# A gate's products spread over the last inverse of a DeltaNet layer, with other pools and planner costs, and an early table load

## The chip, the cores and the metric

The kernel runs on one core of a Trainium2 chip. The metric is the device time of one execution in microseconds. "TensorE" (PE in the profile) does matrix products, "DVE" is VectorE, "ACT" is ScalarE, "POOL" is GpSimd, and "SP" is SyncE, whose queue issues nearly all DMA transfers. PEld is TensorE's weight load, which overlaps its products.

## The reference: what is computed

One layer of a streaming encoder on a sequence of 1024 frames of width 1024, then a final RMSNorm. All is in float32. Cut to what matters:

```python
h = rmsnorm(x, norm_mix_g)
proj = h @ w_in            # columns of all heads, and two merge gates
# Branch A: gated DeltaNet, 8 heads of 128: causal conv + SiLU on q, k, v, chunks of tokens
lower = where(strict, beta * (k k^T) * decay, 0)
sol = triangular_solve(lower, rhs, unit_diagonal=True)      # the kernel forms the inverse itself
# then a scan over the chunks with a state of 128 x 128 per head
# Branch B: GLA, 4 heads, chunked, with its own scan
merged = sigmoid(gate_a) * (o_a @ w_branch_gdn) + sigmoid(gate_b) * (o_b @ w_branch_gla)
x = x + merged @ w_out
# cross attention over 256 memory tokens
m = rmsnorm(mem, norm_mem_g)
k, v = m @ wk, m @ wv
x = x + softmax(q k^T / 16) v @ wo
# MLP
x = x + square(relu(rmsnorm(x) @ w1)) @ w2
return rmsnorm(x, norm_final_g)
```

## The kernel before

**Products.** A float32 operand is split into a rounded part (`hi`, by ACT) and a remainder (`lo`, by DVE or POOL): this is `split` (lines 584 and 585 of the profile). One product of two such operands is then three products of TensorE, `hi*hi`, `hi*lo`, `lo*hi` (`mm3`, lines 544, 546 and 548). Most large products use a scheme of seven products in place of eight on 2 by 2 blocks (`wino`), with operands 0 to 6 that lie in the slots B0a, B0b, A1a, A1b, A0a, B1a, B1b. A few are plain float32 products, which the profile shows as two records each.

**Order.** Two things set it. First, dense products are pushed as generators on a queue (`push`), and dependent work calls `fill(n)` to put the next n dense products at that place of the program, or `until(name)` and `drain()` to put all of them up to a name there. Secondly, a planner (`Plan`, with costs of every operation in `Op`) reads the whole program and fixes an order on each engine: the operation with the least latest start first on DVE, ACT, POOL and SP; on TensorE, of those that are ready, the one that stands first in the program. So a later product can be put into a gap in which the earlier ones aren't ready. The order is fixed before the run; each engine then works strictly through its own. TensorTensor operations with two operands can go to DVE or to POOL, as the planner's costs say.

**Phases.** `phase0` loads the memory tokens (`mem_piece`, line 702: ACT scales each of eight blocks of 256 tokens by the norm's gain into `mf`), forms keys and values and the normalised x. `phase_gla` is branch B. `phase_gdn` is branch A: four pairs of heads p = 0 to 3; each has convolutions of k, q, v (`push_conv`: 48 products, then ACT line 1247, three DVE steps at line 1250 and a SiLU at line 1251), `gdn_subst` on DVE (ending in two transposes, lines 1367 and 1371, into `PF` and `PT`), `gdn_queries`, `gdn_v` (line 616 transposes, line 1427), `gdn_inverse` and `gdn_scan`. `gdn_inverse` is a chain of small products (32 by 32 at lines 1394 and 1403, 64 by 64 at lines 1410 and 1417) with copies by ACT and DVE between them and a `fill(nfill)` at four places. For the first three pairs `nfill` is `GF[6]`, 8, and the queue holds the next pair's convolutions.

For the last pair there is no next pair. The queue ends with gate 5 (`push_gate`: one load of weights, then 48 products in two halves, each with a tanh by ACT and a store). The fills of 24 and 16 behind the two `gdn_v` and then `drain()` put its products in front of the inverse; `ectx.close(); wctx.close()` free the phase's pools; `begin_merge` opens the pools of the merge (`plate`, `big2` with B0a and B0b, `w4` with the weights) and loads the operands 0 to 4 of the first merge product `yb`. Then come the inverse and the scan, and behind them in the program `yb`, of which the planner puts products into the scan's gaps. A slot A1a, A1b, A0a is free for its merge operand only when the gate's products, which read the normalised x in it, are through.

**Pools.** Pools are stacked from both ends of on-chip memory ("left" and "right"); a pool that lies over the addresses of a closed one waits for the last use of what was there. `pge` (right) held k0, kdt0, NT0, dm and acc of the phase; `w1` (right, outside it) holds raw weights and a ring of four split ones (`wop`).

Of the kernel before, what the change touches and what calls it, by code (L numbers as in the profile page):

```python
# [18 lines left out]
P = 128  # L19
# [24 lines left out]
KP = 2  # L44
LOVU = (5,)
LOV = (0, 2, 5)
GLG, GN = 0, (0, 0, 0, 1)
ZA = "z"
DH = ((0, 1, 2, 3), (4, 5, 6, 7), (), ())
XF = (4, 12, 10, 8)  # L50
# [32 lines left out]
class Op:  # L83
# [5 lines left out]
    def __init__(self, ins, flex):  # L89
# [27 lines left out]
        if scan:  # L117
            vec = 65 + wide * 2.08
        elif ins.opcode == "StreamTranspose":
            vec = (830 if rough else 90) + wide * 1.042  # L120
        elif ins.opcode == "Reciprocal" or n <= 16 and wide <= 16:
            vec = 82
        pool = {"Memset": 20 + n * 0.875, "TensorScalarAffineSelect": 140 + n * 0.89, "TensorCopy": 140 + n * 0.9}
        self.costs = costs = {"vector": vec, "gpsimd": 245 + n * 1.98 if sums else pool.get(ins.opcode, 100 + n)}
        if sums and n <= 16:
            costs["gpsimd"] = 330 + 160 * n
        if ins.opcode == "DMACopy":
            self.dma, self.cost, self.lat = True, 60, 2600
            self.bytes = n * 4 * outs[0].ap[0][1]
        elif eng == "tensor":  # L130
            m = size(ins_[0])
            if ins.is_transpose:
                self.cost = m * 0.85
            elif ins_[0].dtype == F32R:
                self.cost = m * 0.4427 + (4 if m < HALF else 0)
            else:
                self.cost = max(m, size(ins_[1])) * 1.667 + 8
            self.lat = 205
        elif eng == "scalar":
            self.cost = (60 if psum(ins_[0]) else 95) + n * (1.71 if rough else 0.834) + 90 * min(cols, 1) + 90 * (len(outs) > 1)  # L140
            self.lat, self.own = 140, 130
        else:
            self.port = eng == "gpsimd" or two
            self.place(eng)

# [320 lines left out]
class Layer:  # L466
# [151 lines left out]

    def slot(self, name, shape=(NB, HALF), dt=F32R):

        pool = self.bp if name[0] == "A" else self.bp2 if name[1] == "0" else self.bp3
        return self.til(pool, (P,) + shape, name, dt, bufs=1)

    def colsum(self, out, src, n):
# [37 lines left out]
    def consts(self):  # L662
        nc, a = self.nc, self.a
        cp = self.cp = self.pool(self.ctx, "const", "left")
        self.ident = self.til(cp, [P, P], "ident")
        make_identity(self.tc.nc, self.ident)
        self.mhalf = self.til(cp, [P, 16], "mhalf")
        nc.vector.memset(self.mhalf, -0.5)
        self.ones = self.til(cp, [P, 1], "ones")
        nc.vector.memset(self.ones, 1.0)  # L670
        cols = self.til(cp, [P, 56], "cols")
        nc.scalar.dma_start(cols, a["cols"])
        self.g_mix, self.g_x = cols[:, 0:8], cols[:, 8:16]
        self.g_mem, self.g_mlp = cols[:, 16:24], cols[:, 24:32]
        self.b_gate, self.g_fin = cols[:, 32:36], cols[:, 48:56]
        self.a_log, self.dt_bias = cols[:, 39:40], cols[:, 40:41]

        gh = self.til(cp, [P, 3], "ghalf")
        nc.vector.tensor_scalar(gh, cols[:, 36:39], 0.5, None, MUL)
        self.g_gdn, self.g_gla = gh[:, 0:1], gh[:, 1:3]  # L680
        self.convw = self.til(cp, [P, 24, 4], "convw")
        nc.sync.dma_start(self.convw, a["convw"])
        self.tm = self.til(cp, [P, NB, 2, GH], "tm")
        self.geg = self.til(cp, [P, NB, GH], "geg")
        self.gge, self.kf = (self.til(cp, [P, GH, NB], n) for n in ("gge", "kf"))
        self.pad(cp, 160)


    def phase0(self, xp, gp):
        nc, a = self.nc, self.a  # L690
        with ExitStack() as ctx:
# [6 lines left out]

            def mem_piece(i):
                self.load(mraw[:, 2 * i:2 * i + 2], a["memT"][:, 2 * i:2 * i + 2])  # L700
                for k in (2 * i, 2 * i + 1):
                    nc.scalar.activation(mf[:, k], mraw[:, k], AF.Copy, scale=self.g_mem[:, k:k + 1])

            def split_mem():
                self.split(mf, mT[:, 0], mT[:, 1], nc.vector)
# [450 lines left out]
    def phase_gla(self):  # L1156
        nc, a = self.nc, self.a
        with ExitStack() as ctx:
# [31 lines left out]
            for h in range(LH):  # L1190
# [31 lines left out]
                self.push_z(sp, h + 1, after if ZA == "z" else None)  # L1222
                if h < LH - 2:
                    self.push_gates(sp, 5 + h)
                if h == LH - 2:
                    for i in range(5, 5 + GLG):
                        self.push_gate(i, lambda src: self.wpart(src, [NB, P], nc.vector), sp, "ex", EXB, T)
                self.fill(FG if h == 1 else FE)


# [294 lines left out]
    def phase_gdn(self, wctx):  # L1525

        nc, a = self.nc, self.a
        with ExitStack() as lctx:
            ectx, sctx = ExitStack(), ExitStack()
            sv = self.pool(lctx, "pgv", "left", bufs=2)  # L1530
            sq = self.pool(sctx, "pgl", "left", bufs=2)
            sp = self.pool(ectx, "pge", "right", bufs=2)
# [1 line left out]
                self.til(sv, [P, T], tag, bufs=2)  # L1534
            for tag in ("k1", "kdt1", "NT1", "q"):
                self.til(sq, [P, T], tag, bufs=2)
            for tag in ("k0", "kdt0", "NT0", "dm", "acc"):
                self.til(sp, [P, T], tag, bufs=2)
            self.til(sq, [P, T], "X", bufs=2)
            self.subTA = self.til(sq, [P, 16, 64], "subTA", bufs=1)  # L1540
            nc.gpsimd.memset(self.subTA, 0.0)
# [2 lines left out]

            def push_keys(hs):
                par = hs[0] // 2 % 2
                sts = [{"pool": sq if par else sp, "tag": lambda t: f"{t}{par}"} for _ in hs]
                for h, st in zip(hs, sts):
                    st["k"] = self.til(st["pool"], [P, NB, P], st["tag"]("k"), bufs=2)
                    conv(f"k{h}", GH + h, a["w_gdn"][3 * h], lambda acc, st=st: st["k"])  # L1550
                return sts
# [6 lines left out]
                self.gdn_keys(sp, sq, hs[1], sts[1])  # L1558
                return self.gdn_subst(sp, sq, sts)

            gates = iter(range(5 + GLG, 6))
            getw = lambda src: self.wpart(src, [NB, P])
            last = None
            sts = push_keys((0, 1))
            for st, h in zip(sts, (0, 1)):
# [1 line left out]
            for p in range(GH // 2):  # L1567
# [9 lines left out]
                nxt = None  # L1577
                if p < GH // 2 - 1:
                    nxt = push_keys((2 * p + 2, 2 * p + 3))
                for _ in range(GN[p]):  # L1580
                    self.push_gate(next(gates), getw, sp)
                if last:
                    for h, st in last:
                        self.gdn_norm(sv, st)
# [9 lines left out]
                self.fill(GF[3])  # L1594
                self.gdn_queries(sv, sp, sts[1])
                self.until(f"v{hs[1]}")
                self.gdn_v(sv, sts[0])
                self.fill(GF[4])
                self.gdn_v(sv, sts[1])
                self.fill(GF[5])  # L1600
                if nxt:
                    self.until(f"k{hs[1] + 2}")
                else:
                    self.drain()
                    ectx.close()
                    wctx.close()
                    ob = self.begin_merge()
                self.gdn_inverse(sts, PF, GF[6])
                if nxt:
                    ns = (2 * p + 2, 2 * p + 3)  # L1610
                    for st, h in zip(nxt, ns):
                        self.load_decay(sp, h, st)
# [16 lines left out]

    def begin_merge(self):  # L1630

        sp = self.plate = self.pool(self.ctx, "plate", "right")
        self.pad(sp, 32, ([P, HALF], "e", 3), ([P, HALF], "acc", 2), ([P, HALF], "q", 4))
        self.bp2 = self.pool(self.ctx, "big2", "right")
        for n in ("B0a", "B0b"):
            self.slot(n)
        self.wp = self.pool(self.ctx, "w4", "right")
        self.queue_w()
        self.fetch_w()
        ob = {"SL": ("B0a", "B0b", "A1a", "A1b", "A0a", "B1a", "B1b")}  # L1640
        for p in range(5):
            self.load_op(sp, ob, p, lambda p, k: self.obd[p][:, k], range(4), None)
        return ob

    def big3(self, ob):

# [1005 lines left out]
```

## Time and profile before

| what | value |
|---|---|
| median of 3 runs | 2131.04 us (2130.86 to 2133.01) |
| the profiled execution | 2133.65 us, span 2131.8 us |
| TensorE's mean granted clock | 0.994 of full speed |
| busy: TensorE, DVE, ACT, POOL | 2105.4, 1694.6, 1124.6, 198.3 us |

The span runs from the first to the last instruction that the profile shows. A row of busy time by stretch has the stretch, its length, then for PE, PEld, DVE, ACT and POOL the busy microseconds and the number of instructions, then TensorE's granted clock as a share of full speed, the mean busy share of the 16 DMA engines, and GB/s. A row of the timeline has start and length in us, engine, line, operation, output and inputs; in brackets the idle time before it and what ended that.

### The profile page before, as it was taken

To read this page: it belongs to the slowest core of one execution; us is meant where nothing else is said; L and a number is where in the kernel's file an instruction comes from. 1 tells how busy PE (TensorE), PEld (TensorE's weight loads), DVE (VectorE), ACT (ScalarE), POOL (GpSimd) and SP (SyncE) were. 2 spreads that over 40 slices of the span, in tenths; PEclk is the share of its full clock that TensorE was granted. 3 is DMA by queue.
4 is the path that set the end of the run, shared out by engine and by line. 5 is a ranking of instruction groups with operands and counts; after the bars stand their busy time and mean duration, and the time that the engine had idled before them with its cause. 6 is when DMAs were issued, how large, how long until landed. Compare 5 with 4: busy or idle time off the path is not lost.

```text
span 2131.8 us, 31725 instructions
## 1 busy us (share of the span) xinstructions
PE 2105.4 (99%) x11308; PEld 1771.7 (83%) x11308; DVE 1694.6 (79%) x3051; ACT 1124.6 (53%) x2244; POOL 198.3 (9%) x199
## 2 busy tenths in 40 slices
PE   8999999999999999999999999999999999999998
PEld 7898887988888888888888888888888888887877
DVE  7979698879768787777899858788979777577766
ACT  6555454454454747475643446676655556444433
POOL 1102001000001121212010001100200000000001
PEclk9999999999999999999999999999999999999999
DMA  7523333223241030303498653466454556688852
GB/s 279 197 70 111 129 120 114 80 89 120 74 140 60 11 124 12 124 11 118 151 307 299 216 198 112 143 198 220 122 157 141 163 158 183 198 276 267 273 180 91
DMA packets 147040, 321.70 MB, mean 151 GB/s; under 512 B 16056, under 2 KB 19512, under 8 KB 146880
## 3 DMA queue, kind: packets, MB, share of 16 engines
q1 hardware_dynamic: 143984, 315.44, 45.1%
q10 hardware_dynamic: 2896, 4.22, 0.6%
q8 instruction: 89, 1.46, 0.3%
q14 instruction: 71, 0.58, 0.1%
HBM read 223.10 MB, written 96.50 MB: 150 GB/s over the span
## 4 chain that ended last, share of the span: by engine, by line
PE 86%; DVE 6%; DMA 3%; ACT 2%; issue 1%; POOL 0%; SPq 0%; POOLq 0%; DVEq 0%; ACTq 0%
PE pd L544 20%; PE pd L546 20%; PE pd L548 20%; PE ps L544 5%; PE ps L546 5%; PE ps L548 5%; PE ps L616 2%; DMA raw<-in_w_dram 1%; DMA rawa<-ad 1%; DMA e<-ad 1%; PE ps L1452 1%; PE pd L767 1%; PE ps L1459 1%; PE ps L1469 1%; PE ps L1311 1%
## 5 line engine op out<-in xcount | busy, mean ns | idle before, releaser
L584 ACT ACTIVATE wop<-raw 128x512 fp32r<-128x512 f32 (+1 forms) x535 | 355.9, 671 | 527.2 <-PE pd L548 253.8
L585 DVE TENSOR_TENSOR wop<-raw,wop 128x512 fp32r<-128x512 f32 (+1 forms) x512 | 373.6, 734 | 122.7 <-ACT wop L584 115.6
L548 PE MATMUL pd<-A1a,wop 128*128 128x512 f32 x376 | 148.6, 395 | 0.0
L544 PE MATMUL pd<-A1a,wop 128*128 128x512 f32 x376 | 147.1, 392 | 0.0
L546 PE MATMUL pd<-A1b,wop 128*128 128x512 f32 x356 | 139.7, 392 | 0.0
L548 PE MATMUL pd<-t,wop 128*128 128x512 f32 x312 | 124.0, 398 | 0.1
L544 PE MATMUL pd<-t,wop 128*128 128x512 f32 x312 | 121.8, 391 | 2.1 <-ACT wop L584 1.9
L546 PE MATMUL pd<-A1a,wop 128*128 128x512 f32 x312 | 122.8, 394 | 0.2
L546 PE MATMUL pd<-t,wop 128*128 128x512 f32 x312 | 121.7, 390 | 0.0
L544 PE MATMUL pd<-A1b,wop 128*128 128x512 f32 x292 | 115.4, 395 | 0.0
L548 PE MATMUL pd<-A1b,wop 128*128 128x512 f32 x292 | 114.7, 394 | 0.0
L1250 DVE SCALAR_TENSOR_TENSOR acc<-cin,convw,acc 128x1024 f32<-128x1024 f32 x72 | 94.4, 1312 | 15.5 <-ACT acc L1248 14.9
L544 PEld LDWEIGHTS pd<-A1a,wop 128*128 128x128 f32 x376 | 70.7, 188 | 14.3
L548 PEld LDWEIGHTS pd<-A1a,wop 128*128 128x128 f32 x376 | 70.7, 188 | 13.9
L544 PE MATMUL pd<-B0a,wop 128*128 128x512 f32 x196 | 77.1, 394 | 2.5 <-ACT wop L584 2.0
L544 PE MATMUL pd<-A0a,wop 128*128 128x512 f32 x196 | 79.4, 405 | 0.0
L546 PEld LDWEIGHTS pd<-A1b,wop 128*128 128x128 f32 x356 | 66.9, 188 | 13.4 <-DVE A1b L585 0.5
L546 PE MATMUL pd<-A0a,wop 128*128 128x512 f32 x196 | 78.0, 398 | 0.0
L548 PE MATMUL pd<-B0a,wop 128*128 128x512 f32 x196 | 77.4, 395 | 0.0
L548 PE MATMUL pd<-A0a,wop 128*128 128x512 f32 x196 | 77.2, 394 | 0.0
L546 PE MATMUL pd<-A0b,wop 128*128 128x512 f32 x184 | 73.2, 398 | 0.0
L548 PE MATMUL pd<-A0b,wop 128*128 128x512 f32 x184 | 72.6, 395 | 0.0
(660 smaller groups left out, 6025.8 us busy)
## 6 DMA issues: line engine op xcount, KB each, us to landing
raw<-in_w_dram SPq DMA_DIRECT2D x120, 256.0 KB, 4.0
raw<-in_w_dram SPq DMA_DIRECT2D x32, 512.0 KB, 4.4
e<-ad SPq DMA_DIRECT2D x63, 256.0 KB, 4.8
raw<-in_w_gdn_dram SPq DMA_DIRECT2D x24, 512.0 KB, 5.5
ad<-q SPq DMA_DIRECT2D x45, 256.0 KB, 4.6
rawa<-ad SPq DMA_DIRECT2D x42, 256.0 KB, 4.7
A0b<-tgd SPq DMA_DIRECT2D x32, 256.0 KB, 5.1
raw<-in_w_gate_dram SPq DMA_DIRECT2D x15, 512.0 KB, 3.7
```

The source lines that it names most:

```text
L544: nc.tensor.matmul(out, lh, rh, start=first and i == 0, stop=False, skip_group_check=more)
L546: nc.tensor.matmul(out, lh, rl, start=False, stop=False, skip_group_check=more)
L548: nc.tensor.matmul(out, ll, rh, start=False, stop=last and i == n - 1, skip_group_check=more)
L584: nc.scalar.activation(hi, raw, AF.Copy)
L585: (lo_eng or nc.gpsimd).tensor_tensor(lo, raw, hi.bitcast(F32), SUB)
L616: self.nc.tensor.transpose(pt[:, i * P:(i + 1) * P], s, self.ident)
L767: nc.tensor.matmul(pt[:, j * MEM:(j + 1) * MEM], w[k // 4][:, k % 4, js], mf[:, k], start=k == 0, stop=k == NB - 1)
L1250: nc.vector.scalar_tensor_tensor(acc, cin[:, 1 + i:1 + i + T], cw[:, i:i + 1], acc, MUL, ADD)
L1311: nc.tensor.matmul(pt[:, i * P:(i + 1) * P], kc, kc, start=True, stop=True)
L1452: nc.tensor.matmul(py[:, 0:P], st["NT"][:, c, :], zh[h], start=True, stop=True)
L1459: nc.tensor.matmul(pd[h][:, 0:P], st["kd"][:, c, :], dl[h], start=True, stop=True)
L1469: nc.tensor.matmul(po[:, 0:P], st["AT"][:, c, :], dl[h], start=True, stop=True)
```

## The change

The costs of some operations in the planner are changed. The gate's products get their fills inside the last inverse (`GL`, four fills of 12), its split weights and its tanh output a pool of their own. k0, kdt0 and NT0 get a pool that closes when the last pair begins. The pools of the merge and its operand 0 are opened in front of the inverse as before, operands 1 to 4, with the slot B0b in a new pool, behind it. At the beginning ACT runs a copy of one column at once, before mem arrives, and DVE scales every second block of mem. The branch with `GLG` in `phase_gla` had an empty range and is taken out.

```diff
-GLG, GN = 0, (0, 0, 0, 1)
+GL = (0,0,12)
...
         elif ins.opcode == "StreamTranspose":
-            vec = (830 if rough else 90) + wide * 1.042
+            vec = 60 + wide * 1.93 if rough else 90 + wide * 1.042
...
-        pool = {"Memset": 20 + n * 0.875, "TensorScalarAffineSelect": 140 + n * 0.89, "TensorCopy": 140 + n * 0.9}
-        self.costs = costs = {"vector": vec, "gpsimd": 245 + n * 1.98 if sums else pool.get(ins.opcode, 100 + n)}
+        pool = {"Memset": 20 + n * 0.875, "TensorScalarAffineSelect": 140 + n * 1.29, "TensorCopy": 300 + n * 2}
+        self.costs = costs = {"vector": vec, "gpsimd": 320 + n * 1.98 if sums else pool.get(ins.opcode, 100 + n)}
...
+            if outs[0].ap[0][1] < P:
+                self.cost += 117
...
+            if eng == "vector" and outs[0].ap[0][1] < P:
+                costs["vector"] += 117
...
-        pool = self.bp if name[0] == "A" else self.bp2 if name[1] == "0" else self.bp3
+        pool = self.bp if name[0] == "A" else self.bp3 if name[1] == "1" else self.bp2 if name == "B0a" else self.bp4
...
         nc.scalar.dma_start(cols, a["cols"])
+        nc.scalar.activation(self.mhalf[:, 15:16], self.ones, AF.Copy)
...
             def mem_piece(i):
                 self.load(mraw[:, 2 * i:2 * i + 2], a["memT"][:, 2 * i:2 * i + 2])
-                for k in (2 * i, 2 * i + 1):
-                    nc.scalar.activation(mf[:, k], mraw[:, k], AF.Copy, scale=self.g_mem[:, k:k + 1])
+                nc.scalar.activation(mf[:, 2 * i], mraw[:, 2 * i], AF.Copy, scale=self.g_mem[:, 2 * i:2 * i + 1])
+                nc.vector.tensor_scalar(mf[:, 2 * i + 1], mraw[:, 2 * i + 1], self.g_mem[:, 2 * i + 1:2 * i + 2], None, MUL)
...
-            for tag in ("k0", "kdt0", "NT0", "dm", "acc"):
+            for tag in ("dm", "acc"):
                 self.til(sp, [P, T], tag, bufs=2)
+            pk = self.pool(kctx, "pgk", "right", bufs=2)
+            for tag in ("k0", "kdt0", "NT0"):
+                self.til(pk, [P, T], tag, bufs=2)
...
-            gates = iter(range(5 + GLG, 6))
-            getw = lambda src: self.wpart(src, [NB, P])
...
                 if p < GH // 2 - 1:
                     nxt = push_keys((2 * p + 2, 2 * p + 3))
-                for _ in range(GN[p]):
-                    self.push_gate(next(gates), getw, sp)
+                else:
+                    kctx.close()
+                    gp = self.pool(gctx, "pgg", "left")
+
+                    def getw(src):
+                        raw = self.til(self.wp, [P, NB, P], "raw", bufs=RAWS)
+                        hi, lo = (self.til(gp, [P, NB, P], n, F32R, bufs=1) for n in ("ghi", "glo"))
+                        self.load(raw, src)
+                        self.split(raw, hi, lo)
+                        return hi, lo
+
+                    self.push_gate(5, getw, gp, "tg", 2)
...
                 self.until(f"v{hs[1]}")
+                if not nxt:
+                    self.fill(1)
                 self.gdn_v(sv, sts[0])
-                self.fill(GF[4])
+                self.fill(GF[4] if nxt else GL[0])
                 self.gdn_v(sv, sts[1])
-                self.fill(GF[5])
+                self.fill(GF[5] if nxt else GL[1])
                 if nxt:
                     self.until(f"k{hs[1] + 2}")
                 else:
-                    self.drain()
                     ectx.close()
                     wctx.close()
                     ob = self.begin_merge()
-                self.gdn_inverse(sts, PF, GF[6])
-                if nxt:
+                self.gdn_inverse(sts, PF, GF[6] if nxt else GL[2])
+                if not nxt:
+                    self.drain()
+                    gctx.close()
+                    self.begin_ops(ob)
+                else:
...
     def begin_merge(self):
...
-        for n in ("B0a", "B0b"):
-            self.slot(n)
+        self.slot("B0a")
...
-        for p in range(5):
-            self.load_op(sp, ob, p, lambda p, k: self.obd[p][:, k], range(4), None)
+        self.load_op(self.plate, ob, 0, lambda p, k: self.obd[p][:, k], range(4), None)
         return ob
+
+    def begin_ops(self, ob):
+
+        self.bp4 = self.pool(self.ctx, "big4", "right")
+        for p in range(1, 5):
+            self.load_op(self.plate, ob, p, lambda p, k: self.obd[p][:, k], range(4), None)
```

More of the change, by code (lines that the diff above doesn't have):

```diff
@@ L1224, in phase_gla @@
                     self.push_gates(sp, 5 + h)
-                if h == LH - 2:
-                    for i in range(5, 5 + GLG):
-                        self.push_gate(i, lambda src: self.wpart(src, [NB, P], nc.vector), sp, "ex", EXB, T)
                 self.fill(FG if h == 1 else FE)
@@ L1528, in phase_gdn @@
         with ExitStack() as lctx:
-            ectx, sctx = ExitStack(), ExitStack()
+            ectx, sctx, kctx, gctx = (ExitStack() for _ in range(4))
             sv = self.pool(lctx, "pgv", "left", bufs=2)
@@ L1546, in push_keys @@
                 par = hs[0] // 2 % 2
-                sts = [{"pool": sq if par else sp, "tag": lambda t: f"{t}{par}"} for _ in hs]
+                sts = [{"pool": sq if par else pk, "tag": lambda t: f"{t}{par}"} for _ in hs]
                 for h, st in zip(hs, sts):
@@ L1630, in begin_merge @@
     def begin_merge(self):
-        sp = self.plate = self.pool(self.ctx, "plate", "right")
-        self.pad(sp, 32, ([P, HALF], "e", 3), ([P, HALF], "acc", 2), ([P, HALF], "q", 4))
+        self.plate = self.pool(self.ctx, "plate", "right")
+        self.pad(self.plate, 32, ([P, HALF], "e", 3), ([P, HALF], "acc", 2), ([P, HALF], "q", 4))
         self.bp2 = self.pool(self.ctx, "big2", "right")
-        for n in ("B0a", "B0b"):
-            self.slot(n)
+        self.slot("B0a")
         self.wp = self.pool(self.ctx, "w4", "right")
```

## The prediction

> **What bounds the kernel.** I read the page first, then TensorE's waits, then the busy time by stretch, and last the timeline of the two places that the diff touches.
>
> ```profile
> PE 2105.4 (99%) x11308; PEld 1771.7 (83%) x11308; DVE 1694.6 (79%) x3051; ACT 1124.6 (53%) x2244; POOL 198.3 (9%) x199
> PE 86%; DVE 6%; DMA 3%; ACT 2%; issue 1%; POOL 0%; SPq 0%; POOLq 0%; DVEq 0%; ACTq 0%
> PE pd L544 <- ACT wop L584: 6.7, 5, 2.2
> PE pd L767 <- ACT mf L702: 1.6, 1, 1.6
> PE ps L1410 <- DVE subTA L1404: 1.5, 1, 1.5
> ```
>
> TensorE is busy 99% of the span and is 86% of the chain that ended last. The diff takes no product away, so the change can pay only where TensorE stands idle or runs at a lower clock. Of the waits listed (us in total, times, longest), the third lies in the last inverse, one of the five of the first as well, and the second at the beginning: the change reaches those.
>
> The clock is the larger matter. These rows (TensorE's clock behind the POOL column, as a share of full speed) cut the time around the last inverse into stretches of 3.41 us:
>
> ```profile
> 991.40:1003.90 12.50, 12.50 (x65) 10.36 (x63) 8.83 (x9) 2.84 (x4) 3.02 (x2) 1.00 0.25 84
> 1003.90:1005.05 1.15, 1.15 (x34) 0.87 (x34) 0.00 (x0) 0.76 (x2) 0.10 (x1) 1.00 0.00 0
> 1005.05:1008.46 3.41, 1.83 (x89) 1.59 (x84) 1.28 (x3) 3.17 (x9) 0.00 (x0) 1.00 0.77 232
> 1008.46:1011.87 3.41, 2.88 (x64) 2.63 (x64) 0.56 (x2) 2.40 (x6) 0.00 (x0) 0.50 0.96 383
> 1011.87:1015.28 3.41, 1.98 (x10) 1.33 (x11) 3.35 (x6) 1.75 (x4) 0.00 (x0) 0.50 0.60 206
> 1015.28:1018.70 3.42, 3.42 (x38) 3.42 (x37) 1.80 (x4) 1.74 (x3) 0.00 (x0) 0.50 0.37 111
> 1018.70:1022.12 3.42, 3.42 (x17) 2.92 (x16) 1.89 (x3) 0.89 (x2) 0.00 (x0) 0.50 0.00 0
> ```
>
> Until 1003.9 the gate's 48 products keep TensorE full. Then the inverse stands bare: 1.58 + 0.53 + 1.43 = 3.54 us idle, and four stretches, 13.66 us, at half clock. The first three inverses, against the last:
>
> ```profile
> 698.20:711.10 12.90, 12.90 (x248) 10.68 (x247) 8.28 (x11) 9.08 (x18) 0.10 (x1) 1.00 0.11 38
> 803.70:816.60 12.90, 12.90 (x248) 10.75 (x248) 8.28 (x11) 9.08 (x18) 0.10 (x1) 1.00 0.13 40
> 909.10:922.10 13.00, 13.00 (x248) 10.81 (x248) 8.31 (x12) 9.08 (x18) 0.10 (x1) 1.00 0.12 41
> 1004.20:1020.40 16.20, 12.67 (x229) 11.22 (x229) 7.89 (x15) 9.81 (x21) 0.05 (x1) 0.63 0.57 196
> ```
>
> An inverse has 32 + 48 + 16 + 16 small float32 products in the code, which leave two records each, 224 in all; a dense product leaves one. The first three have 24 dense products between its steps (three fills of 8), TensorE full and the clock whole; the last has five, and 0.63.
>
> **The change, part by part.** *The gate's products beside the inverse.* Same 48 products, same place in the dense queue; only the fills move: none behind the two gdn_v, then four times 12 in the inverse. The weights are still requested before it. A dense product takes the step between these two starts, 0.23 us:
>
> ```profile
> 1003.41 0.39 PE L544 MATMUL pd<-A1a,wop 128*128 128x512 f32 x1
> 1003.64 0.39 PE L546 MATMUL pd<-A1a,wop 128*128 128x512 f32 x1
> ```
>
> So an inverse's own work at full clock is 12.9 - 24 x 0.23 = 7.4 us. Now 1004.2 to 1020.4 holds that and five products of the merge: 7.4 + 5 x 0.23 = 8.55 us of work in 16.2 us. That is 7.65 us to win, and half of the 1.72 us at half clock from 1020.4 to 1022.12, 0.86: **8.5 us**, if TensorE stays full from 991.4. A second way, all half-clock busy time counted half: 3.54 + 11.70 / 2 = 9.4, the upper end. The lower end is the idle time alone, 3.5. I take 8.5, since three inverses with this cover show it.
>
> Is the work there to be interleaved? Behind the last convolution's products (until 991.4) stands its chain on DVE and ACT:
>
> ```profile
> 991.38 1.07 DVE L1367 STREAM_TRANSPOSE X<-Pm 128x512 f32<-128x512 f32 x1
> 995.19 1.06 DVE L1371 STREAM_TRANSPOSE X<-X 128x512 f32<-128x512 f32 x1
> 999.30 1.06 ACT L1251 ACTIVATE acc<-acc 128x1024 f32<-128x1024 f32 x1 [0.85 <-DVE acc L1250]
> 1000.41 1.09 PE L616 MATMUL ps<-ident,acc 128*128 128x128 f32 x8
> ```
>
> The gate now hides that chain until 1000.4. With the gate's products spread out, the cover is the inverse itself: its first operand exists at 992.45 and its second transpose, put behind a convolution step at 995.19, at 996.25 even if it isn't moved forward. In the worst case some 20 products (4.6 us / 0.23) go before the inverse really starts; 28 are left, more than the 24 that sufficed three times. DVE has 17.7 us of work in 991.4 to 1022.12 (the seven rows), 79% of the 22.2 us that remain, its mean over the span; ACT 13.55, 61%. So neither becomes the bound there. Scan start moves from 1020.4 to about 1012.
>
> *Pools.* k0, kdt0 and NT0 get a pool that closes before the last pair; the split gate weights get a pool of their own and no longer pass through the four-deep weight ring. That lets the merge's weights and B0a be opened before the inverse. Against it: the operand in B0b opens only when the gate's last product and tanh are through, near 1012, and its ACT splits wait for that with the scan's evictions behind them on ACT. Cost taken as zero, because the scan had other work first:
>
> ```profile
> 1020.41 0.63 PE L1452 MATMUL ps<-v,NT 128*128 128x128 f32 x2
> 1032.31 0.39 PE L544 MATMUL pd<-B0b,wop 128*128 128x512 f32 x1
> 1022.12:1053.20 31.08, 31.08 (x208) 27.49 (x208) 28.75 (x74) 25.39 (x84) 1.45 (x2) 1.00 0.39 129
> 1022.12:1053.20 31.08, 19.89 (x63) 10.65 (x64) 2.06 (x3) 1.21 (x2) 1.00 0.39 129
> ```
>
> The last row is the dense products alone: 63 in the scan. B0b was first read 11.9 us after the scan's start; from 1012 that is 1024, 12 us after the pool opens. Its four loads and the twelve of the operands behind it are issued behind the inverse on SP's queue instead of before it; they had 9 us of lead on the scan and now have about none. If the cover is gone, see the last rival. A gain can come too: B0a ready early.
>
> *Durations.* The planner's costs change for DVE's transposes, short-partition copies and POOL's work; no instruction gets faster by that, but every engine's order from end to end is drawn anew. What it can move is the stalls elsewhere, the largest of them here, where an idle 2.23 us costs half of the next 3.42 us too:
>
> ```profile
> 1940.30:1943.71 3.41, 1.18 (x6) 0.68 (x5) 2.13 (x4) 1.24 (x3) 0.00 (x0) 1.00 0.98 299
> 1943.71:1947.13 3.42, 3.42 (x9) 2.68 (x10) 3.42 (x6) 2.05 (x5) 0.00 (x0) 0.50 0.79 267
> ```
>
> That stall is worth 2.2 + 1.7 = 3.9 us. It may go, or another like it may come: plus or minus 3.9, taken as zero.
>
> *The beginning.*
>
> ```profile
> 4.12 1.28 ACT L702 ACT_TABLE_LOAD   x1 [4.12 <-DMA mraw<-in_memT_dram]
> 5.42 1.71 ACT L702 ACTIVATE mf<-mraw,cols 128x256 f32<-128x256 f32 x4
> 5.98 1.13 PE L767 MATMUL pd<-mf,raw 128*128 128x256 f32 x4 [1.55 <-ACT mf L702]
> 8.47 3.81 PE L767 MATMUL pd<-mf,raw 128*128 128x256 f32 x9 [1.36 <-DMA raw<-in_wk_dram]
> 9.96 0.69 DVE L733 TENSOR_TENSOR mraw<-mraw 128x512 f32<-128x512 f32 x1 [2.12 <-ACT mf L702]
> 10.30 0.91 ACT L702 ACTIVATE mf<-mraw,cols 128x256 f32<-128x256 f32 x2 [0.37 <-DMA mraw<-in_memT_dram]
> ```
>
> The load of 1.28 us goes in front of mem's arrival, so the first products start some 1.2 us earlier. But the next ones wait for weights until 8.47: late next is that DMA, and most is lost again. The last mem piece lands at 10.30 and its two scalings (0.91) now run side by side: 0.45 earlier for what follows. DVE gets four scalings of at most 0.69 each, in its waits. I take **0.4 us**, between 0 and 1.3 (the load's 1.28).
>
> **Sum.** 8.5 + 0.4 = 8.9 us. The profiled execution took 2133.65 us (span 2131.8), 2.6 above the median of the three runs, 2131.04; I take the gain off the median: 2131.0 - 8.9 = **2122.1 us**.
>
> **Rivals.** (a) Only the idle time comes back: 2131.0 - 3.5 - 0.4 = 2127.1. For it: 1015.28 to 1022.12 was full and still at half clock, so small products may hold it down. Against it: the three inverses at 1.00. The Trainium skill, "TensorE: Matmul & The Clock Gate", Part 1, says that the clock halves after at least one idle window of about 3.4 us. The rows disagree: 1.83 us of 3.41 busy was followed by half clock, without an idle window. By the Trainium skill alone the bare inverse would not have halved the clock, hence the halving would not hang on its gaps, and one would expect 2127.1. Chance 0.13.
>
> (b) DVE gives half of it back. Behind the scan it has no idle time left:
>
> ```profile
> 1053.20:1119.20 66.00, 66.00 (x301) 54.82 (x300) 62.75 (x109) 29.52 (x54) 13.66 (x6) 1.00 0.88 296
> 1119.20:1185.00 65.80, 65.80 (x292) 54.47 (x291) 65.18 (x107) 26.80 (x47) 2.86 (x2) 1.00 0.91 312
> ```
>
> DVE is busy 62.75 of 66.0 and 65.18 of 65.8 us. Against it: TensorE is at 66.0 and 65.8, so DVE's backlog was never what it waited for, and 8.9 us less of DVE's idle time before the scan is only lost if operands are then readier now than later. Half of 8.9: 2126.6. Chance 0.13.
>
> (c) It doesn't do what it says: the gate's products run out while the last convolution's chain is pending (until 1000.4, 9.0 us or 39 products) and nine are left for the inverse, as now: about 2130.6. Against it: the operand ready at 992.45. Chance 0.07.
>
> (d) Slower: B0b is starved. B0a has 24 products, about 12 us of the scan by 63 in 31 us; if B0b and the operand after it come only behind the scan, the other 39 are missing, 9.0 us idle, and with half clock over the remaining 19 us the scan's own work there ((31.08 - 63 x 0.23) x 19 / 31 = 10.1 us) can cost up to as much again; with half of that, 14 us, 2131 - 8.9 + 14 = 2136. It decides from 8.9 us lost, B0b later than about 16 us behind the point where B0a is used up. Chance 0.07.
>
> **Chances and range.** Forecast 0.60, with its own range 2118 to 2126 (the stall of 3.9 either way). A change of 0.2%, 4.3 us, is about what can be told from none: faster is under 2126.8. Faster: 0.60 and two thirds of (b), 0.69; same, with (a), (c) and the rest of (b), 0.24; slower 0.07. The range reaches to (a) with a little: 2117.5 to 2128.5, leaving out (c), (d) and small ends.
>
> **What would show it.** The clock at 1.00 from 991 on; the inverse's products among dense ones on A1b and A1a; scan start near 1012; no ACT table load behind 4 us; the first product of mem near 4.8. Wrong would be: half clock in the inverse; an idle TensorE in the scan with B0b as its releaser; new stalls behind 1185.

## The result, and the profile after

The changed kernel takes 2115.98 us (median of six, 2115.49 to 2119.57) against 2131.39 us (six, 2130.60 to 2133.01): a ratio of 0.9931, 95% interval 0.9918 to 0.9944. It is faster by 15.4 us, where 8.9 had been forecast, and lies 1.5 us below the low end of the range.

The page of the changed kernel, its busy times and its chain, then three of TensorE's waits (us in all, times, longest):

```profile
PE 2098.1 (99%) x11308; PEld 1768.0 (84%) x11308; DVE 1692.7 (80%) x3068; ACT 1124.5 (53%) x2241; POOL 172.0 (8%) x186
PE 95%; DVE 2%; DMA 1%; issue 1%; ACT 1%; SPq 0%; DVEq 0%; POOLq 0%; ACTq 0%
PE pd L552 <- DVE wlo L589: 1.5, 2, 1.1
PE pd L772 <- DMA raw<-in_wk_dram: 1.4, 2, 0.8
PE pd L548 <- ACT wop L588: 0.7, 1, 0.7
```

The chain is now 95% TensorE, 86% before. Of the first group of before's waits, five on a split by ACT with 6.7 us, one of 0.7 is left, and the wait inside the inverse is gone. Between its first and its last product TensorE is idle for 5.6 us, 15.8 before; 4.3 of the 5.6 stand in the first 45 us, and behind them no gap is longer than 0.4. (Lines moved a little: L544, L546, L548 are now L548, L550, L552, and the inverse's L1394 is L1396.)

Busy time by stretch, first after, then the two late places of before that the prediction did not show in full:

```profile
985.00:1108.00 123.00, 123.00 (x818) 103.11 (x817) 111.23 (x222) 68.73 (x167) 9.69 (x7) 1.00 0.64 218
999.30:1013.14 13.84, 13.84 (x251) 11.15 (x250) 11.71 (x22) 10.27 (x21) 0.00 (x0) 1.00 0.57 211
1922.00:1942.00 20.00, 20.00 (x90) 16.57 (x89) 15.27 (x24) 9.74 (x17) 0.00 (x0) 1.00 0.96 327
2030.00:2050.00 20.00, 20.00 (x90) 16.44 (x89) 16.72 (x27) 7.10 (x12) 3.61 (x3) 1.00 0.58 193
```

```profile
1936.00:1956.00 20.00, 17.77 (x71) 14.15 (x70) 12.20 (x19) 7.59 (x13) 0.00 (x0) 0.91 0.89 285
2040.00:2060.00 20.00, 18.51 (x82) 14.83 (x82) 17.84 (x28) 8.20 (x13) 4.50 (x3) 1.00 0.67 216
```

The whole of 985 to 1108 has TensorE full at clock 1.00; the inverse takes 13.84 us there (16.2 before). And the stalls that before has near 1941 and 2049 are not there at all.

Where the time came from: the start of the same product in both traces, after minus before. The profiled executions differ by more than the medians do (2115.65 against 2133.65, so 18.0), because the one of before stood 2.3 above its median.

| at (us, before) | difference | what lies in between |
|---|---|---|
| 23 | 0.0 | the new beginning |
| 186 | -1.0 | the stall of 0.39 near 177 |
| 386 | -2.8 | the stall of 0.99 near 328 |
| 991 | -2.5 | |
| 1020 (scan start) | -7.3 | the inverse |
| 1154 | -10.2 | scan and first merge product |
| 1876 | -10.8 | |
| 2001 | -15.7 | the stall of 2.23 and its half clock near 1941 |
| 2114 | -17.5 | the stall of 1.49 near 2049 |

From 991 to 1154, the place that the change is about, come 7.7 us. The other ten come from places that the diff does not name.

What stood beside the inverse was not what had been planned. Rows of the timeline after: two of DVE and ACT, then TensorE.

```profile
988.65 1.07 DVE L1369 STREAM_TRANSPOSE X<-Pm 128x512 f32<-128x512 f32 x1
996.92 1.66 ACT L588 ACTIVATE B0a<-e 128x512 fp32r<-128x512 f32 x3
...
989.58 0.48 PE L548 MATMUL pd<-A0a,ghi 128*128 128x512 f32 x1
...
998.09 0.40 PE L548 MATMUL pd<-A1b,ghi 128*128 128x512 f32 x1
998.33 1.04 PE L620 MATMUL ps<-ident,acc 128*128 128x128 f32 x8
999.30 1.98 PE L1396 MATMUL ps<-X,NT 32*32 32x32 f32 x64
1001.21 0.50 PE L550 MATMUL pd<-A1b,ghi 128*128 128x512 f32 x1
...
1004.46 0.39 PE L552 MATMUL pd<-A1a,glo 128*128 128x512 f32 x1
1004.69 0.40 PE L548 MATMUL pd<-B0a,wop 128*128 128x512 f32 x1
...
1013.14 0.49 PE L1454 MATMUL ps<-v,NT 128*128 128x128 f32 x2
```

The operand `ghi`, `glo` is the gate. Its products run from 989.58 to 998.33 with nothing between them: 37 of the 48 are gone before the inverse's first product at 999.30, although the inverse's operand was transposed at 989.72. The first step of the inverse stands right behind the eight transposes L620 of the second `gdn_v`. Eleven gate products are left, and from 1004.69 on the cover is the merge: 14 products on B0a, whose splits on ACT ran at 996.92, in before only at 1011.06:

```profile
1011.06 1.67 ACT L584 ACTIVATE B0a<-e 128x512 fp32r<-128x512 f32 x3
1005.28 2.78 SPq L504 DMA_DIRECT2D raw<-in_w_bgla_dram  x4
```

The second row is SP's queue in before, the issue of the merge's weights; after it stands earlier:

```profile
996.47 1.88 SPq L508 DMA_DIRECT2D raw<-in_w_bgla_dram  x4
```

### The profile page after: what moved, and what is told of

It is laid out like the page before. It is cut to its first block, busy times and chain, and to the rows that moved or that the text cites. A ratio compares the mean times of both kernels' runs of the same rounds, so it can differ in the third digit from the quotient of the medians.

```text
span 2113.9 us, 31742 instructions
## 1 busy us (share of the span) xinstructions
PE 2098.1 (99%) x11308; PEld 1768.0 (84%) x11308; DVE 1692.7 (80%) x3068; ACT 1124.5 (53%) x2241; POOL 172.0 (8%) x186
## 4 chain that ended last, share of the span: by engine, by line
PE 95%; DVE 2%; DMA 1%; issue 1%; ACT 1%; SPq 0%; DVEq 0%; POOLq 0%; ACTq 0%
PE pd L550 22%; PE pd L548 22%; PE pd L552 22%; PE ps L548 6%; PE ps L552 6%; PE ps L550 6%; PE ps L620 2%; PE pd L772 1%; PE ps L1454 1%; PE ps L1471 1%; PE ps L1461 1%; PE ps L1313 1%; PE ps L1327 1%; PE ps L1116 1%; PE ps L1444 1%; PE ps L1445 1%
## 5 line engine op out<-in xcount | busy, mean ns | idle before, releaser
L552 PE MATMUL pd<-A1a,wop 128*128 128x512 f32 x372 | 147.1, 395 | 0.0
L548 PE MATMUL pd<-A1a,wop 128*128 128x512 f32 x372 | 146.5, 394 | 0.0
L550 PE MATMUL pd<-A1b,wop 128*128 128x512 f32 x352 | 138.7, 394 | 0.0
L552 PE MATMUL pd<-t,wop 128*128 128x512 f32 x312 | 123.7, 397 | 0.0
L548 PE MATMUL pd<-t,wop 128*128 128x512 f32 x312 | 121.8, 391 | 0.2 <-ACT u L1922 0.2
L550 PE MATMUL pd<-t,wop 128*128 128x512 f32 x312 | 121.6, 390 | 0.0
L550 PE MATMUL pd<-A1a,wop 128*128 128x512 f32 x308 | 121.4, 394 | 0.1
L552 PE MATMUL pd<-A1b,wop 128*128 128x512 f32 x288 | 113.6, 394 | 0.0
L548 PE MATMUL pd<-A1b,wop 128*128 128x512 f32 x288 | 112.8, 392 | 0.0
L548 PEld LDWEIGHTS pd<-A1a,wop 128*128 128x128 f32 x372 | 69.9, 188 | 13.9 <-ACT A1a L588 0.3
L552 PEld LDWEIGHTS pd<-A1a,wop 128*128 128x128 f32 x372 | 69.9, 188 | 13.7
L548 PE MATMUL pd<-A0a,wop 128*128 128x512 f32 x192 | 77.6, 404 | 0.0
L550 PEld LDWEIGHTS pd<-A1b,wop 128*128 128x128 f32 x352 | 66.1, 188 | 13.3
L550 PE MATMUL pd<-A0a,wop 128*128 128x512 f32 x192 | 76.8, 400 | 0.0
L552 PE MATMUL pd<-B0a,wop 128*128 128x512 f32 x196 | 76.6, 391 | 0.0
L548 PE MATMUL pd<-B0a,wop 128*128 128x512 f32 x196 | 76.4, 390 | 0.0
L552 PE MATMUL pd<-A0a,wop 128*128 128x512 f32 x192 | 75.8, 395 | 0.0
L550 PE MATMUL pd<-A0b,wop 128*128 128x512 f32 x180 | 71.0, 395 | 0.0
L552 PE MATMUL pd<-A0b,wop 128*128 128x512 f32 x180 | 70.9, 394 | 0.0
```

Source lines behind the costliest of these rows:

```text
L548: nc.tensor.matmul(out, lh, rh, start=first and i == 0, stop=False, skip_group_check=more)
L550: nc.tensor.matmul(out, lh, rl, start=False, stop=False, skip_group_check=more)
L552: nc.tensor.matmul(out, ll, rh, start=False, stop=last and i == n - 1, skip_group_check=more)
```

## The experiments

Each ratio is against the kernel before, run beside it on the same chip, with its 95% interval. In the expectations, theory A is that the gate's fills inside the inverse are its cover; theory B is that operand B0a, let in early by the new pools, is.

**The gate put ahead of the inverse again.** All else as after.

```diff
-GL = (0,0,12)
+GL = (24,24,0)
```

> The changed kernel with GL = (24, 24, 0) in place of (0, 0, 12): the gate's 48 products stand in front of the last inverse in the program again, pools, costs and beginning as changed. Theory A (the gate's products are the cover): the inverse is bare, some 3 us idle and up to four windows at half clock come back, +5 to +8 us against the changed kernel, 2121 to 2124. Theory B (the cover is the merge's first products, which the early pools let in, 14 of them stood there against 10 of the gate's): 0 to +2 us, 2116 to 2118, clock 1.00 in the inverse.

2118.59 us, 0.9943 [0.9931, 0.9956]: 2.6 us slower than after. The inverse, without one gate product beside it:

```profile
1002.66:1016.33 13.67, 13.19 (x245) 10.13 (x244) 10.52 (x18) 12.31 (x25) 1.28 (x1) 1.00 0.50 171
```

The clock stays whole, idle is 0.48 us, and 20 products on B0a do the covering. So A's number fell: the clock at the inverse doesn't need the fills inside it, after which the change is named. Without them the kernel loses 2.6 us of the 15.4 by the medians, whose intervals overlap; product by product 2.8 lie at the inverse.

**The merge's pools opened behind the inverse in the program.**

```diff
-                else:
-                    ectx.close()
-                    wctx.close()
-                    ob = self.begin_merge()
...
                     gctx.close()
+                    ectx.close()
+                    wctx.close()
+                    ob = self.begin_merge()
                     self.begin_ops(ob)
```

> The changed kernel with begin_merge (and the closing of the phase's pools) moved behind the inverse, fills of 12 kept. Theory A: the gate's products alone cover the inverse, 0 to +1 us, 2116 to 2117. Theory B: some 11 gate products are left when the inverse starts, not enough; idle and half clock in the second half of the inverse and in the scan's beginning, where B0a is late now: +4 to +9 us, 2120 to 2125.

2116.87 us, 0.9932 [0.9918, 0.9946]: as after, so B's number fell. But the edit did not move what it was meant to move:

```profile
998.76:1012.59 13.83, 13.83 (x250) 11.13 (x249) 11.70 (x22) 10.27 (x21) 0.00 (x0) 1.00 0.57 213
```

The same 25 products stand beside the inverse, and B0a is split at 996.38, as early as after. The planner can put a load as early as its addresses are free; the place of `begin_merge` in the program did not hold it back. This run tests the text's order, not B.

**The gate's weights back in the old ring.** As the first experiment, and the split through the four-deep ring. This does move B0a.

```diff
-GL = (0,0,12)
+GL = (24,24,0)
...
-                        raw = self.til(self.wp, [P, NB, P], "raw", bufs=RAWS)
-                        hi, lo = (self.til(gp, [P, NB, P], n, F32R, bufs=1) for n in ("ghi", "glo"))
-                        self.load(raw, src)
-                        self.split(raw, hi, lo)
-                        return hi, lo
+                        return self.wpart(src, [NB, P])
```

> The changed kernel with GL = (24, 24, 0) and the gate's weights split into the old ring (wpart) in place of their own pool. Theory B2 (what covers the inverse is B0a's products, and they can start early because nothing of the gate holds the old ring's addresses): they come behind the inverse's middle again, some 3 us idle and half clock, 2122 to 2126 (2118.6 with the own pool). If the ring doesn't matter: 2118.6 within 1.5.

2126.31 us, 0.9979 [0.9970, 0.9989]: 7.7 us slower than the first experiment, from which only the ring differs.

```profile
1000.26:1015.43 15.17, 12.95 (x234) 10.39 (x233) 10.94 (x19) 11.07 (x23) 0.07 (x1) 0.78 0.55 189
PE ps L1412 <- DVE subTA L1406: 1.4, 1, 1.4
...
1007.28 0.61 ACT L588 ACTIVATE B0a<-e 128x512 fp32r<-128x512 f32 x1
```

The wait of before inside the inverse is back, 2.2 us are idle, the clock is half for 6.83 us, and B0a is split seven microseconds after the inverse began, not before it. Product by product it loses 3.5 us from the inverse to 1147. The rest of the 7.7 isn't placed: the profiled execution of this kernel stood 2.1 below its median, that of the first experiment 2.9 above, so that only 2.7 us lie between the two. With the gate put ahead, this is B in its working form: it is the freed ring that lets the cover in. The pool of k0, kdt0 and NT0, which this kernel keeps, does not do it alone; whether it is needed was not tried.

**The parts alone.** Only the gate and its pools; only the costs; only the beginning; everything but the beginning; everything but the costs.
Costs alone, on before, and below it the beginning alone, on before; the other three kernels are the changed one with these hunks undone. "The ledger" in the expectations is the table of differences above.

```diff
-            vec = (830 if rough else 90) + wide * 1.042
+            vec = 60 + wide * 1.93 if rough else 90 + wide * 1.042
...
-        self.costs = costs = {"vector": vec, "gpsimd": 245 + n * 1.98 if sums else pool.get(ins.opcode, 100 + n)}
+        self.costs = costs = {"vector": vec, "gpsimd": 320 + n * 1.98 if sums else pool.get(ins.opcode, 100 + n)}
...
```

```diff
+        nc.scalar.activation(self.mhalf[:, 15:16], self.ones, AF.Copy)
...
+                nc.vector.tensor_scalar(mf[:, 2 * i + 1], mraw[:, 2 * i + 1], self.g_mem[:, 2 * i + 1:2 * i + 2], None, MUL)
```

Costs alone:

> The kernel before with the planner's changed costs alone. The ledger of the two traces has about 9 us in stalls far from the edits (1.8 near 330 us, 4.9 near 1941, 1.7 near 2049, about 1 elsewhere). Theory C (the corrected costs take these stalls away): 2131 - 6 to 9 = 2122 to 2125, the inverse still at half clock. Theory D (the stalls went because any change draws the order anew; the costs have no direction): anything from 2127 to 2135, the stalls elsewhere.

Gate and pools alone:

> The kernel before with the gate's fills and the pools alone: old costs, old beginning. The inverse is worth 7.6 us in the ledger, so 2131 - 7.6 = 2123.5 (2122 to 2125) if the costs take away the other stalls (theory C), with the waits near 330, 1941 and 2049 still there. Theory D: 2116 to 2128, with other stalls.

All but the beginning:

> The changed kernel with the old beginning (no early table load, ACT scales all of mem). Theory C2 (gate and pools are worth 6 us by themselves, and the new costs take the waits near 176 and 328 us away once more, while the late ones go or come with the order): 2116 to 2119, the beginning worth 0 to 1 us. Theory S (the beginning is worth the missing part): 2122 to 2126, as with the gate and pools alone.

The beginning alone:

> The kernel before with the beginning alone (early table load, DVE scales every second block). The ledger has the two traces level at 23.7 us, so 0: 2131.5 within 1 us, if the order behind stays. Theory S: 2122 to 2126. Theory D: the redrawn order moves it by some us either way, with the place of the move far behind 55 us.

All but the costs:

> The changed kernel with the old costs (gate, pools and beginning new). Theory C3 (the costs): 2123 to 2131, like the four runs with old costs and new pools (2125.7 to 2132.0). Theory S2 (the beginning, in this order): 2115 to 2120.

| kernel | median us | ratio |
|---|---|---|
| gate and pools | 2125.72 | 0.9974 [0.9963, 0.9985] |
| costs | 2131.76 | 0.9999 [0.9990, 1.0007] |
| beginning | 2131.97 | 1.0005 [0.9995, 1.0014] |
| gate, pools and costs | 2118.12 | 0.9938 [0.9926, 0.9951] |
| gate, pools and beginning | 2124.52 | 0.9970 [0.9958, 0.9982] |

The parts do not add up: 5.8 + 0 + 0 is not 15.4. Of the gate and pools alone, the inverse and three waits; of the costs alone, the inverse and its two longest:

```profile
1000.21:1013.50 13.29, 12.75 (x248) 10.57 (x248) 11.58 (x21) 9.94 (x22) 0.00 (x0) 1.00 0.63 234
PE pd L544 <- ACT u L1917: 1.4, 1, 1.4
PE pd L544 <- DVE u L1878: 1.3, 1, 1.3
PE ps L1111 <- DVE v L1121: 1.0, 1, 1.0
```

```profile
1002.00:1019.00 17.00, 13.99 (x196) 11.78 (x190) 8.87 (x16) 9.71 (x21) 0.62 (x1) 0.55 0.53 187
PE pd L548 <- ACT wop L588: 5.2, 4, 2.9
PE ps L1414 <- DVE subTA L1408: 1.5, 1, 1.5
```

The gate with its pools makes the inverse whole (6.1 us from 991 to 1147 in its trace) but keeps stalls elsewhere. The costs leave the inverse as bad as it was, and trade the stalls of before for others: one of 2.9 us now. The beginning alone is worth nothing that can be told; three pairs of kernels with the new pools that differ by it alone lie 1.2 to 2.3 us apart in its favour, with intervals that overlap. The gate and its pools came out 0.7 us above theory C's end and inside theory D's range. Theory C fell with the costs alone, theory S with the beginning alone and with all but the beginning, and S2 with all but the costs, whose 2124.5 us lie where C3 had put them.

What covers the inverse in the kernel with the gate and its pools is not what covers it after. Its dense products between 1000.30 and 1012.44 that read `ghi`, then those that read `glo`, then the first product on B0a:

```profile
1000.30:1012.44 12.14, 3.52 (x10) 1.80 (x10) 0.00 (x0) 0.00 (x0) 1.00 0.64 239
1000.30:1012.44 12.14, 2.40 (x6) 1.13 (x6) 0.00 (x0) 1.00 0.64 239
1012.59 0.47 PE L544 MATMUL pd<-B0a,wop 128*128 128x512 f32 x1
```

Sixteen products of the gate stand there and none on B0a, and the clock is whole. So it is in all five kernels with the new pools and the old costs (one of them has a single product on B0a). Theory A's cover is thus enough without B's, as B's was without A's in the first experiment: either will do. (The fills with the old ring were not run.) From 991 to 1154, product by product against before, the traces with both gain 6.5 to 7.7 us, those with the gate's sixteen 5.5 to 6.6, the one with B0a alone 4.8, and those with the old ring between 1.3 and a loss of 1.6.

**The order drawn again.** If what is left is the planner's order as such, then a planner's constant moved by 2 ns for every instruction of DVE, or the assumed latency of a DMA by 100 ns, must move the time as much, though no engine works differently by it. This was done to before, to the gate with its pools ("gate") and to the full change.

The first and the second redraw; the third is the first with 63 in place of 67.

```diff
-        vec = 65 + wide * 1.042 + 58 * min(cols, 1)
+        vec = 67 + wide * 1.042 + 58 * min(cols, 1)
```

```diff
-            self.dma, self.cost, self.lat = True, 60, 2600
+            self.dma, self.cost, self.lat = True, 60, 2700
```

Before, first redraw, then second and third:

> The kernel before with one planner constant moved by 2 ns (DVE's 65 to 67), no work moved. Theory D (every redraw of the order moves the stalls in the last 250 us by several us): a time that differs from 2131.5 by 1.5 to 5 us either way, with other stalls behind 1180 us. Theory C: 2131.5 within 1 us.

> The kernel before with the planner's DMA latency 2700 in place of 2600. A second width for the draw: theory L, 2127 to 2137 with other stalls behind 1180 us; the inverse still at half clock. If the first redraw's 5 us was peculiar: 2131 within 1.5 us.

> The kernel before, DVE's constant 63: the level for the others. So far 2131, 2136.2 and 2125.6 by draw; 2124 to 2137, the last inverse idle and at half clock as in all kernels with the old pools.

Gate and pools, first, second and third:

> The gate's fills and pools alone (old costs, old beginning, 2125.7 us) with DVE's planner constant 67. Theory L: anything from 2118 to 2130. Theory C3: 2123 to 2130, with the waits near 176 and 328 us there, which cost 2.4 us in the ledger.

> Gate's fills and pools alone, old costs, DMA latency 2700. Its twin with the new costs and the new beginning took 2117.8. Theory C3 (the new costs keep stalls away): 2123 to 2130. Theory L (draw): 2115 to 2130, and in one of the two old-cost runs of this set at or below its twin.

> Gate's fills and pools alone, old costs, DVE's constant 63. Theory C3: 2123 to 2130, above its twin with new costs by 3 us or more. Theory L: 2115 to 2130, either side of it.

The full change, first, second and third, and the third without the new beginning:

> The changed kernel with DVE's planner constant 67 in place of 65, no work moved. Theory L (2116 is a lucky draw of the order; the stalls behind 1180 us come back with the next one): 2118 to 2124. Theory C3 (the new costs keep stalls away in any draw): 2115 to 2118.

> The changed kernel with the planner's DMA latency 2700 in place of 2600, no work moved. Theory L: 2118 to 2124; theory C3: 2115 to 2118.

> The changed kernel, DVE's constant 63. Theory C3: 2115 to 2119 (the 2130.5 with 67 was the outlier). Theory L: 2116 to 2130.

> The changed kernel with the old beginning and DVE's constant 63. Theory C3: 2116 to 2121. Theory S2: 2123 to 2131. By draw alone: anything from 2116 to 2131.

| median us (ratio to before) | as it is | first | second | third |
|---|---|---|---|---|
| before | 2131.4 | 2136.2 (1.0021 [1.0012, 1.0030]) | 2125.6 (0.9975 [0.9965, 0.9985]) | 2137.4 (1.0021 [1.0011, 1.0030]) |
| gate | 2125.7 | 2128.0 (0.9985 [0.9977, 0.9994]) | 2132.0 (1.0000 [0.9990, 1.0009]) | 2127.8 (0.9979 [0.9969, 0.9988]) |
| full change | 2116.0 | 2130.5 (0.9993 [0.9984, 1.0002]) | 2117.8 (0.9939 [0.9927, 0.9951]) | 2119.3 (0.9938 [0.9923, 0.9952]) |

Without the new beginning the third gives 2121.6 (0.9953 [0.9937, 0.9969]). Each against the kernel before beside it (whose median was 2131.1 to 2132.6 us), an edit without content moves before by -5.6 to +5.1 us and takes 2.0 to 14.7 us of the full change's 15.4. With the first redraw the full change has lost its whole gain, and not at the inverse:

```profile
999.00:1013.50 14.50, 14.50 (x257) 11.64 (x255) 12.29 (x22) 11.04 (x24) 0.00 (x0) 1.00 0.58 216
1184.45:1187.62 3.17, 0.01 (x1) 0.00 (x0) 3.17 (x7) 1.20 (x3) 0.00 (x0) 1.00 0.00 0
1188.74:1195.57 6.83, 6.12 (x14) 4.81 (x15) 4.96 (x9) 1.23 (x2) 0.00 (x0) 0.50 0.85 281
1945.73:1948.82 3.09, 0.01 (x1) 0.01 (x1) 2.01 (x4) 0.92 (x3) 0.00 (x0) 1.00 0.69 227
1949.91:1953.33 3.42, 3.42 (x10) 2.64 (x9) 3.24 (x6) 1.31 (x3) 0.00 (x0) 0.50 0.94 318
```

The inverse is the good one, whole and at clock 1.00. At 1184.45 TensorE stands empty for 3.17 us, with DVE full, and two stretches of half clock follow; at 1945.73 it stands empty for 3.09, and one follows. The first of these stalls is two instructions of ACT in the other order. In this kernel, then in the changed one as it is:

```profile
1186.42 0.63 ACT L588 ACTIVATE B0a<-u 128x512 fp32r<-128x512 f32 x1 [2.45 <-DVE u L2010]
1186.96 0.61 ACT L588 ACTIVATE B0a<-e 128x512 fp32r<-128x512 f32 x1
```

```profile
1182.95 0.61 ACT L588 ACTIVATE B0a<-e 128x512 fp32r<-128x512 f32 x1
1187.79 0.63 ACT L588 ACTIVATE B0a<-u 128x512 fp32r<-128x512 f32 x1 [3.19 <-DVE u L2010]
```

The split of `e` was put behind the split of `u`, for which ACT waits 2.45 us on DVE. In the changed kernel ACT waits for `u` even longer, 3.19 us, but with `e` already done, and TensorE is idle there for 0.16 us only. The gate with the second constant has a stall of 3.5 us in the same place. In the best draw of before, the second, the late stalls are gone while the inverse is as bare as ever:

```profile
1003.00:1019.50 16.50, 12.99 (x236) 11.63 (x235) 8.96 (x16) 10.28 (x22) 0.54 (x2) 0.69 0.55 193
PE ps L1410 <- DVE subTA L1404: 3.5, 2, 1.9
```

Two things follow. What the pools do at the inverse holds in every draw: the clock there is half for 6.8 to 17.1 us in all seven kernels with the old ring, and whole in all thirteen with the gate's own pool. And the rest changes with the draw by as much as is to be explained. Over the four columns the means are 2132.6, 2128.4 and 2120.9 us, so the full change is worth 11.7 us over these draws, with single differences from 5.7 to 18.1.

Of the redraws of before, the first lies where theory D had put it, the second 1.4 us below the range of theory L, the third 0.4 above its range. The first redraw of the full change, 2130.5, missed theories L and C3 alike, and so did the second of the gate, 2132.0. C3 held in the second of the full change and in the first and third of the gate; the third of the full change came out 0.3 us above C3's end, and without the beginning 0.6 above.

Whether the new costs give a better order on the average, given the new pools, stays open, but more speaks for it than against it. With them the six kernels have a mean of 2120.6, without them the five have 2127.6, and five of the six lie below all five. Three pairs that differ by the costs alone are 6.2, 7.6 and 8.5 us apart. Up to 991 us the trace of a kernel with the new costs is ahead of that of its twin with the old ones in each of the four draws, by 1.0 to 4.2 us; but it is one trace of each, and in two draws the twin has the old beginning too. Against it: the sixth kernel lies at 2130.5, 2.5 above the gate in the same draw, and in the old pools the costs gave nothing.

## Why the prediction was right or wrong

- **The bound** was right: what was won is idle time, 10.2 us less in the span, and half-clock time: the five stretches of the prediction's rows held 15.1 us of work, counted at half 7.6 us. Together 17.8 of the 17.9 us between the two spans, but that they meet is in part luck: at the inverse this count gives 9.4 us, and 7.7 were measured; 1.0 of the 10.2 lies in the first 45 us, where it moved nothing; and a sixth stretch at half clock, at the beginning of before, is left out and cost nothing (below).
- **The inverse**, 8.5 us between 3.5 and 9.4: 7.7 measured from 991 to 1154. The size was right to 0.8. (Of the "five products of the merge" in the bare inverse one was the gate's last; that moves the sum by 0.2.) The scan starts at 1013.1, about 1012 had been said; the clock is 1.00 from 991 on.
- **How it comes about** was wrong in half. "In the worst case some 20 products go before the inverse really starts": it was 37. The step took the operand's readiness for the start. In the trace the inverse's first products come behind the transposes L620 of `gdn_v` in all of these kernels; both write TensorE's result tiles of the one kind `ps`, and I take it that these are used in the program's order. That reason was not tested. So rival (c) was right on the gate's products, with eleven left, not nine, and wrong on the time, because the pools let B0a in. With the old costs sixteen were left, and they covered the inverse without B0a. "Pools", taken as zero with the remark "a gain can come too: B0a ready early", is a term of its own at the inverse: with the new costs the ring is worth 3.5 us and the fills another 2.8 of the 7.7.
- **Durations**: "plus or minus 3.9, taken as zero". This is the step that failed. 15.4 less 7.7 leaves 7.7 us, which are this term (10.2 in the trace, whose before was 2.3 above its median). The prediction took the largest stall for the end of it. But a new order can drop every stall, and TensorE's idle time outside the beginning and the inverse was 7.0 us in before, with 1.7 us of half clock behind the one at 1941: 8.7 us would have been a better end on that side. On the other side no row of before gave an end, and the first redraw took 14.7. How much of the 7.7 is the new costs' own and how much the luck of the draw stays open. Some of it is luck: of the four draws of the full change this one is the fastest, and their mean of 2120.9 us lies inside the range and 1.2 below the forecast.
- **The beginning**, 0.4 us between 0 and 1.3: nothing. The load of the table is gone from mem's way and the first product starts 0.77 us earlier, yet the products behind it end level, at 19.38 and 19.40. What was late next is weights by DMA, as the prediction had said. In before a stretch there runs at half clock, 8 records against 9 after, with the DMA engines full in both, and even that cost nothing. Rows after, then before:

```profile
1.25 1.28 ACT L677 ACT_TABLE_LOAD   x1 [1.25 <-PEq L2656]
5.21 2.05 PE L772 MATMUL pd<-mf,raw 128*128 128x256 f32 x4 [0.79 <-DMA raw<-in_wk_dram]
7.83 11.55 PE L772 MATMUL pd<-mf,raw 128*128 128x256 f32 x42 [0.56 <-DMA raw<-in_wk_dram]
8.36:11.77 3.41, 3.41 (x9) 2.70 (x8) 2.89 (x5) 2.54 (x3) 0.00 (x0) 1.00 1.04 408
```

```profile
8.47 10.93 PE L767 MATMUL pd<-mf,raw 128*128 128x256 f32 x42 [1.36 <-DMA raw<-in_wk_dram]
8.36:11.77 3.41, 3.30 (x8) 2.71 (x9) 1.23 (x2) 2.35 (x5) 0.00 (x0) 0.50 1.04 380
```

- **The rivals.** (a), only the idle time: fell, the clock came back whole. (b), DVE gives half back behind 1185: not in this draw. The first redraw has a stall at 1184, with DVE busy 3.17 of 3.17 us; there DVE's backlog counts only because ACT's order was worse. (d), B0b starved: not seen; of 985 to 1108 TensorE is idle for nothing.

## What to carry to other kernels

Where a planner fixes the whole order, a change in its costs, or in anything that it reads, is also a new draw: price it by the sum of all stalls of the kernel before on the gain side, not by the largest, and measure the spread by moving a constant that means nothing, on both kernels, before a gain of that size is credited to an idea. Look for cover by asking which operands can be in memory by then as well as by moving fills: here an operand let in early by a freed ring, and sixteen of the gate's products, each kept the clock whole without the other. What is robust shows in every draw at the same place of the trace.

## What the runs showed of the hardware

The clock falls in whole stretches of 3.41 us, and a stretch need not be idle for that: before 1008.46, 1.83 of 3.41 us were busy, before 1943.71, 1.18 (both in the prediction's rows). What a stall costs does not follow from its length: 2.23 us idle at 1941 in before and 1.87 at 1424 in the first redraw of the full change were followed by half clock; 2.79 at 1951 in the third redraw of before, 1.98 at 1939.88 with the old ring and 1.49 at 2049 in before were not. Where it lies plays a part: the 1.98 us fell into two stretches, which were busy for 2.57 and 2.27 of 3.41 us. But the busy time of a stretch doesn't settle it either. The stretch with the 1.87 us was busy for 1.55 us, and half clock followed. These two, in the third redraw of before and the first of the full change, were busy for 1.51 and 1.82 us, the second less than the 1.83 before 1008.46, and the clock stayed whole behind them (their limits are counted in steps of 3.413 us from another fall of the clock in the same trace):

```profile
1950.02:1953.44 3.42, 1.51 (x7) 0.94 (x5) 2.45 (x4) 0.63 (x1) 0.00 (x0) 1.00 0.58 224
2048.90:2052.31 3.41, 1.82 (x8) 0.90 (x6) 3.41 (x6) 1.15 (x2) 1.75 (x2) 1.00 0.75 269
```

What decides stays open. So a stall of 1.5 to 3 us costs either itself or itself and 1.7 us for each stretch at half clock behind it; and in before at 8.36, where the DMA engines were full, half clock cost nothing. And at half clock a stretch that is full, but of the inverse's small products, did not lift it; the next, with the last of them, the merge's and the scan's first, did. Rows of before, the last of them behind the prediction's:

```profile
1022.12:1025.54 3.42, 3.42 (x25) 2.97 (x25) 2.73 (x9) 2.58 (x9) 0.00 (x0) 1.00 0.00 0
```

The stretch 1015.28 to 1018.70 was busy 3.42 of 3.42 us at 0.50, and 1018.70 to 1022.12 still ran at 0.50. The Trainium skill, "TensorE: Matmul & The Clock Gate", Part 1, gives the window as 3413 ns and one busy window as enough to warm up; the length agrees with the rows, the rule for warming does not agree with this one, if the window's busy time is what the profile counts.
